# A streaming encoder trunk on one core: the memory's row statistic moved behind the key and value products, and the gated unit, one block and one opening rearranged

## The chip, the core and the metric

One Trainium2 chip, of which the kernel uses one core. The core has TensorE (PE in the profile, with its weight load PEld), VectorE (DVE), ScalarE (ACT), GpSimd (POOL) and SyncE (SP), which issues the transfers. The metric is the time of one execution on the device in microseconds (us), as the median of several runs.

## What is computed

Two layers on 512 tokens of width 1024, all in float32. Layer 0 feeds two branches from one projection (a diagonal complex state space followed by a gated linear unit, and a causal convolution followed by a LayerNorm). Layer 1 is an attention over chunks of 64. Each layer is followed by a cross attention with 4 heads into 256 memory tokens. The parts that the change touches:

```python
def rms_norm(x, g):
    y = xf * lax.rsqrt(jnp.mean(xf * xf, axis=-1, keepdims=True) + EPS)
    return (y * g).astype(x.dtype)

def s5_mixer(u, ...):
    ...
    y = y.reshape(bsz, L, S5_WIDTH) + d_skip * uf
    z = jax.nn.gelu(y)
    return z * jax.nn.sigmoid(z @ glu_w + glu_b)          # glu_w: 512 x 512

def mem_cross_attention(h, mem_n, w_qg, w_kv, w_o):
    q, g = jnp.split(h @ w_qg, 2, axis=-1)
    k, v = jnp.split(mem_n @ w_kv, 2, axis=-1)            # mem_n: 256 x 1024, k and v 256 x 1024 each
    ...

def reference(x, mem, mem_norm_g, ...):
    mem_n = rms_norm(mem, mem_norm_g)
    for layer in range(DEPTH):
        ...
        x = x + ssm_conv_layer(...)  or  chunk_attention_layer(...)
        x = x + mem_cross_attention(rms_norm(x, xa_norm_g[layer]), mem_n, ...)
    return rms_norm(x, final_norm_g)
```

## The kernel before

Activations lie with the width on the 128 partitions and the tokens in the free dimension: a width of 1024 is eight tiles of 128x512, memory eight tiles of 128x256.

**Products.** Nearly every large product takes float32 operands apart into a high part in fp32r and a rest (`split`, L173: the cast to the high part on ACT, the subtraction that gives the rest on POOL, or on the engine that is handed in). `weights` (L178) loads a weight tile through one of three `raw` buffers and splits it into one of two `whi` and one of three `wlo` buffers. `mm3` (L192) then multiplies high by high, high by low and low by high, so that a projection of 1024 rows onto 128 columns (`proj`, L201) is 24 matmuls, the sixteen on `whi` first and the eight on `wlo` after them. Two places use native float32 matmuls instead (`whole`, L187): the gated unit and three of layer 0's eight key tiles (`NATIVE`, L705). The trace writes each native matmul as two records. All matmuls are issued at L82.

**PSUM.** Banks are handed out by tag (L127): three for `proj`, two for `att`, two for `tr`, one for `acc`. A matmul group that takes a bank waits until what was in it has been read.

**Layer 0** is a list of stages (`PLAN`, L706), each a letter and a number: u is a state block's input, z and c the gate and value of a convolution block, g one of eight gates, a, b, o the preparation, scan and output of a state block, k the convolution's taps on DVE for block 0 (four a stage, L823, in a `proj` bank that stays taken throughout), v the taps of blocks 1 to 3 on PE (also in a `proj` bank), m and n the sums and the statistic of memory, l and s the LayerNorm's. The list sets priorities. Within it the scheduler may let an instruction pass another on its engine. `state_input(3)` (L865) is u3; `conv_input(2)` (L805) is c2.

**End of layer 0** (L927 to L977). `zs` are the four inputs of the gated unit. `mem_norm` (L632) spreads the memory's row statistic over the partitions (`bcast`, a matmul of `dg` with `ones` into the `acc` bank), loads the memory a second time, multiplies it by the statistic on DVE, and splits it. Then come the gated unit (four groups of four native matmuls; sigmoid on ACT, product with `zs` on POOL, product with the gate on DVE, split on POOL), the LayerNorm's application (`ln_apply`), and the key and value tiles of cross attention 0 (`kv_units`, L663; order in `KVORDER`, L704: a key tile is one weight tile, a value tile two), then the output projection (`residual`).

**Layer 1.** The chunk attention's projections (`od_qkg_d`, `unit`) are generators that are run between the steps of the attention; PE's order there is pinned. Its opening runs the first two units, takes the row statistic of x after the first (`norm["rs"]`, `dg` on DVE), spreads it with a matmul after the second (`rb_tile`, L279 copies it on ACT), and multiplies queries and keys by it before the first scores. After the chunk attention `mem_norm` runs once more for cross attention 1.

Of the kernel before, what the change touches and what calls it, by code (L numbers as in the profile page):

```python
# [44 lines left out]
def kernel(  # L45
# [578 lines left out]
    def mem_load():  # L624
        st = Stats(MEM)
        for i in range(KT):
            t = tl("mt", (P, MEM))
            nc.sync.dma_start(t, memT_d[i])
            st.add(t, pin=True)
        return st  # L630

    def mem_norm(rs, tag, raw_tag=None):  # L632
        mm, raw = [], []
        with tc.high_priority():
            rbm = bcast(rs, MEM)
# [935 lines left out]
```

## Time and profile before

| what | value |
|---|---|
| median of 3 runs | 984.75 us (981.59 to 985.48) |
| the profiled execution | 984.45 us |
| its span, first to last instruction | 982.5 us |
| mean granted clock of TensorE in it | 0.987 |
| busy: PE, PEld | 948.6 us (97%), 809.9 us (82%) |
| busy: DVE, ACT, POOL | 582.6 us (59%), 467.8 us (48%), 441.2 us (45%) |
| moved by DMA | 110.05 MB, mean 112 GB/s |

An engine is busy while it runs an instruction; waiting is the rest. PE's share is an upper bound of its work, since a matmul that runs slowly under a lowered clock is busy for longer. "Granted clock" is the share of full speed that the chip allowed TensorE in a stretch, 1.00 being 2.4 GHz and 0.50 being 1.2 GHz. Rows of a timeline give start, duration, engine, line, operation, output and inputs, shape and count; in brackets the idle time of that engine just before the row, with what ended it.

### The profile page before, as it was taken

The page shows a single profiled execution, that of the slowest core. Times are in us where ns is not written, and L with a number is a line of the kernel's source. Part 1 is how long each engine was busy: PE and PEld are TensorE (multiplying, and loading weights), DVE is VectorE, ACT ScalarE, POOL GpSimd, SP SyncE. Part 2 cuts the span into 40 slices and gives each one's busy share as a digit, 9 for nine tenths or more (in the row PEclk, how much of TensorE's full clock was granted, in tenths as well). Part 3 has the DMA queues.
Part 4 walks back from the last instruction along what each step waited for, and adds up shares of the span by engine and source line. Part 5 has one row for each costly group of instructions (what it writes and reads, how often), then busy time and mean ns, then how long its engine had stood idle before and what let it go on. Part 6 is the DMA issues. An engine that isn't in the chain of part 4 may idle for free.

```text
span 982.5 us, 14196 instructions
## 1 busy us (share of the span) xinstructions
PE 948.6 (97%) x5256; PEld 809.9 (82%) x5256; DVE 582.6 (59%) x1404; ACT 467.8 (48%) x844; POOL 441.2 (45%) x245
## 2 busy tenths in 40 slices
PE   8998999989999999999999999999999999999996
PEld 7787989758888888888798887878788998888895
DVE  7999746883344343552568777688667313433476
ACT  7243446474443434434366555656545443343352
POOL 1013343059676344457454434444327983434241
PEclk9998999999999999999999999999999999999998
DMA  8253555356422222122222222222114552122153
GB/s 294 100 163 111 166 178 179 101 166 230 161 97 90 82 70 81 65 96 89 84 77 86 82 74 70 75 79 72 65 45 139 171 179 101 65 86 85 44 171 109
DMA packets 50245, 110.05 MB, mean 112 GB/s; under 512 B 11137, under 2 KB 22529, under 8 KB 50177
## 3 DMA queue, kind: packets, MB, share of 16 engines
q1 hardware_dynamic: 49888, 109.07, 33.2%
q8 instruction: 41, 0.67, 0.3%
q14 instruction: 28, 0.22, 0.1%
q10 hardware_dynamic: 288, 0.08, 0.0%
HBM read 103.37 MB, written 5.77 MB: 111 GB/s over the span
## 4 chain that ended last, share of the span: by engine, by line
PE 34%; DVE 10%; ACT 3%; issue 2%; POOL 1%; DMA 1%; POOLq 0%; DVEq 0%; ACTq 0%
PE ps_proj L82 27%; PE ps_att L82 2%; PE ps_tr L85 2%; DVE pe L159 2%; DVE ps_att L1301 1%; PE ps_acc L82 1%; DVE o L154 1%; ACT whi L174 1%; DVE h L163 1%; PE ps_tr L82 1%; ACT pe L1288 1%; POOL wlo L154 1%; DVE z L154 1%; DVE s L1300 1%; DVE qk L154 1%
## 5 line engine op out<-in xcount | busy, mean ns | idle before, releaser
L154 POOL TENSOR_TENSOR wlo<-raw,whi 128x1024 fp32r<-128x1024 f32 x130 | 317.1, 2443 | 412.3 <-ACT whi L174 378.5
L82 PE MATMUL ps_proj<-h,whi 128*128 128x512 f32 x1184 | 301.7, 400 | 5.6 <-DVE x L154 3.3
L82 PEld LDWEIGHTS ps_proj<-h,whi 128*128 128x128 f32 x1184 | 220.6, 191 | 51.5 <-issue 8.0
L174 ACT CAST whi<-raw 128x1024 fp32r<-128x1024 f32 x148 | 155.2, 1049 | 192.2 <-PE ps_proj L82 87.0
L82 PE MATMUL ps_proj<-h,wlo 128*128 128x512 f32 x592 | 151.5, 393 | 0.0
L82 PE MATMUL ps_proj<-og,whi 128*128 128x512 f32 (+1 forms) x672 | 134.9, 347 | 0.5 <-DVE og L154 0.5
L82 PEld LDWEIGHTS ps_proj<-h,wlo 128*128 128x128 f32 x592 | 110.7, 189 | 23.0 <-issue 0.5
L82 PEld LDWEIGHTS ps_proj<-og,whi 128*128 128x128 f32 x672 | 107.6, 188 | 18.0 <-DVE og L154 2.0
L82 PE MATMUL ps_proj<-og,wlo 128*128 128x512 f32 (+1 forms) x344 | 73.4, 348 | 0.1
L82 PEld LDWEIGHTS ps_proj<-og,wlo 128*128 128x128 f32 x344 | 56.1, 188 | 8.8 <-POOL wlo L154 0.4
L154 DVE TENSOR_TENSOR pt<-ps_tr,pt 128x512 fp32r<-128x512 f32 (+1 forms) x80 | 39.9, 526 | 34.8 <-ACT pt L174 34.6
L174 ACT CAST pt<-ps_tr 128x512 fp32r<-128x512 f32 (+1 forms) x80 | 34.1, 460 | 48.2 <-PE ps_tr L85 48.0
L1288 ACT ACTIVATE pe<-ps_att,s 128x128 f32<-128x128 f32 (+3 forms) x64 | 33.4, 525 | 37.7 <-DVE s L168 34.0
L159 DVE TENSOR_SCALAR_CACHE_REDUCE pe<-pe,s 128x256 f32<-128x256 f32 (+3 forms) x96 | 48.5, 521 | 1.8
L154 DVE TENSOR_TENSOR kv<-ps_proj,kv 128x256 fp32r<-128x256 f32 (+1 forms) x24 | 12.3, 511 | 62.9 <-ACT kv L174 62.0
L154 DVE TENSOR_TENSOR z<-ps_proj,rb 128x512 f32<-128x512 f32 x32 | 22.0, 689 | 45.3 <-PE ps_proj L82 45.2
L154 POOL TENSOR_TENSOR sa<-sa,sq 128x512 f32<-128x512 f32 (+1 forms) x28 | 39.1, 1395 | 19.6 <-ACT sq L234 18.3
L154 DVE TENSOR_TENSOR x<-ps_proj,x 128x512 f32<-128x512 f32 (+1 forms) x38 | 22.9, 602 | 41.4 <-PE ps_proj L82 41.4
L163 DVE SCALAR_TENSOR_TENSOR h<-x,par,h 128x512 fp32r<-128x512 f32 x24 | 38.6, 1616 | 13.5 <-ACT h L253 13.5
L85 PE MATMUL ps_tr<-ident,pe 128*128 128x128 f32 x224 | 34.2, 274 | 3.3 <-DVE pe L159 2.3
L85 PEld LDWEIGHTS ps_tr<-ident,pe 128*128 128x128 f32 x224 | 26.9, 140 | 10.0 <-DVE pe L159 4.2
L82 PE MATMUL ps_proj<-whi,h 128*128 128x256 f32 x256 | 33.7, 284 | 0.0
(251 smaller groups left out, 1462.1 us busy)
## 6 DMA issues: line engine op xcount, KB each, us to landing
raw<-in_xa_qg_dram SPq DMA_DIRECT2D x32, 512.0 KB, 3.5
raw<-in_od_qkg_dram SPq DMA_DIRECT2D x24, 512.0 KB, 3.5
raw<-in_xa_o_dram SPq DMA_DIRECT2D x22, 512.0 KB, 3.5
raw<-in_w_in_dram SPq DMA_DIRECT2D x18, 512.0 KB, 4.1
raw<-in_xa_k_dram SPq DMA_DIRECT2D x16, 512.0 KB, 3.8
raw<-in_xa_v_dram SPq DMA_DIRECT2D x16, 512.0 KB, 3.5
cw<-in_cw_dram SPq DMA_DIRECT2D x24, 320.0 KB, 3.2
x<-in_xT_dram SPq DMA_DIRECT2D x16, 256.0 KB, 4.6
```

The costliest lines, as they stand in the source:

```text
L82: return self.keep(nc.tensor.matmul(*args, **kw))
L85: return self.keep(nc.tensor.transpose(*args))
L154: (eng or V).tensor_tensor(out, a, b, op=op)
L159: V.tensor_scalar(out=out, in0=in0, scalar1=s, scalar2=None, op0=op, op1=ALU.add, accum_out=small(1))
L163: V.scalar_tensor_tensor(out=out, in0=a, scalar=s, in1=b, op0=op0, op1=op1)
L174: A.copy(hi, src)
L1288: A.activation(st_["pe"][i], ps[:, c:c + n], AF.Exp, bias=nb, accum_out=st_["sums"][:, i:i + 1])
L1300: V.reduce_max(init, ps[:, :nf], axis=AX.X)
L1301: V.tensor_tensor_reduce(out=ps[:, nf:n], in0=ps[:, nf:n], in1=st["tz"][:, MEM - (n - nf):], scale=1.0, scalar=init, op0=ALU.add, op1=ALU. ...
```

## The change

It has six parts. **Memory** keeps no normalised copy: the tiles are loaded once for layer 0, two to a transfer, and split with the gain alone in a new stage `w0`. The row statistic is applied to the keys, one multiplication of 128x256 on DVE before the split (`kt`), and to the values, as a scalar of each token's row inside the split. For layer 1 the tiles are loaded once more and split, with no statistic. **The gated unit and the three native key tiles** use `weights` and three products; the unit's weights are split on DVE, its inputs are split too (`zp`), and its first product runs on DVE. **The order**: two value and four key tiles (`KVFIRST`) stand ahead of the unit, and the rests of layer 0's key and value weights alternate between POOL and DVE. **u3** takes a bank of `tr`. **The chunk opening**: the first three units' rests come from DVE, and the matmul that spreads the statistic is issued behind the second unit's 16th matmul. **`zs`** is written in place.

```diff
@@ proj
-    def proj(w, act, n=SEQ, cuts=()):
-        ps = psum("proj")
+    def proj(w, act, n=SEQ, cuts=(), tag="proj"):
+        ps = psum(tag)
@@ mem_load, mem_norm
-    def mem_norm(rs, tag, raw_tag=None):
...
-                t = tl("mt", (P, MEM))
-                nc.sync.dma_start(t, memT_d[i])
-                tt(t, rbm, t, ALU.mult)
...
+    def mem_load(tag, st=None):
+        tiles = []
+        for i in range(0, KT, 2):
+            t = tl(tag, (P, 2, MEM))
+            nc.sync.dma_start(t, memT_d[i:i + 2].rearrange("i p s -> p i s"))
+            for e in range(2):
+                if st is not None:
+                    st.add(t[:, e], pin=True)
+                tiles.append(t[:, e])
+        return tiles
+
+    def mem_parts(tiles, his, los):
+        mm = []
+        for i, t in enumerate(tiles):
+            if i % 2 == 0:
+                hi, lo = rl(his[i // 2], (P, 2, MEM)), rl(los[i // 2], (P, 2, MEM))
+            mm.append(gsplit(t, pc("mem_g", i), hi[:, i % 2], lo[:, i % 2]))
+        return mm
@@ kv_units
-            if ("k", i) in native:
-                w = whole(xa_k_d[layer, i])
...
+            ps = proj(weights(xa_k_d[layer, i], eng=eng()), mm, n=MEM)
             e = rl("kv", (P, 2, MEM))
+            t = tl("kt", (P, MEM))
             with tc.high_priority():
-                split(ps[:, :MEM], e[:, 0], e[:, 1], V)
+                tt(t, ps[:, :MEM], mem["rb"], ALU.mult)
+                split(t, e[:, 0], e[:, 1], V)
...
             with tc.high_priority():
-                split(ps.rearrange("p (m c) -> p m c", m=2), hi, lo, V)
+                for t in range(2):
+                    c = slice(t * MEM, (t + 1) * MEM)
+                    gsplit(ps[:, c], mem["rs"][:, t:t + 1], hi[:, t], lo[:, t])
@@ layer 0
-    KVORDER = [('k', 2), ('k', 0), ('k', 1), ('v', 3), ('k', 4), ('v', 0), ('k', 6), ('k', 3), ('k', 5), ('v', 2), ('v', 1), ('k', 7)]
-    NATIVE = [('k', 0), ('k', 1), ('k', 2)]
-    PLAN = "... a2 m0 g4 b2 v3 v3 v3 v3 g5 o2 a3 b3 n0 g6 l0 s0 o3 g7"
+    KVFIRST = [('v', 0), ('k', 0), ('k', 1), ('v', 1), ('k', 2), ('k', 3)]
+    KVORDER = [('v', 2), ('k', 4), ('k', 5), ('v', 3), ('k', 6), ('k', 7)]
+    PLAN = "... a2 m0 g4 b2 w0 v3 v3 v3 v3 g5 o2 a3 b3 n0 g6 l0 s0 o3 g7"
-        ps = proj(weights(w_in_d[3], eng=V), h0) if i == 3 else third if i == 2 else first_ps[i]
+        ps = proj(weights(w_in_d[3], eng=V), h0, tag="tr") if i == 3 else third if i == 2 else first_ps[i]
...
+        rb = bcast(mem["rs"], MEM)
+        mem["rb"] = sm.tile([P, MEM], F32, name="rbm")
+        A.copy(mem["rb"], rb)
+
+    def mem_split(i):
+        mem["mm"] = mem_parts(mem.pop("x"), ["ev"] * 4, ["uu", "x", "x", "x"])
@@ end of layer 0
-    mm, mraw = mem_norm(mrs, "og", "uu")
+    run, kv0 = kv_units(0, mem["mm"], (G, V))
+    for kind, i in KVFIRST:
+        run[kind](i)
...
+    zp = [split(t, rl("og"), rl("og"), V) for t in zs]
     for i in range(4):
-        w = whole(glu_w_d[i], 4)
-        ps = psum("proj")
-        for k in range(4):
-            T.matmul(ps, w[:, k, :], zs[k], start=(k == 0), stop=(k == 3))
-        sg = tl("ev")
+        ps = proj(weights(glu_w_d[i], kt=4, eng=V), zp)
+        sg = tl("sq")
         A.activation(sg, ps, AF.Sigmoid, bias=pc("glu_b", i))
-        tt(sg, zs[i], sg, ALU.mult, G)
-        o = tl("ev")
+        tt(sg, zs[i], sg, ALU.mult)
+        o = gates[i]
...
@@ chunk attention
+            if at is not None and i == at[0]:
+                at[1]()
...
-            for t in unit(od_qkg_d[1], h, keep):
+            def wide():
+                norm["rb"] = rb_tile(norm["rs"])
+
+            for t in unit(od_qkg_d[1], h, keep, eng=V, at=(15, wide)):
                 yield t
-            norm["rb"] = rb_tile(norm["rs"])
...
-            return ("g", hp), unit(od_qkg_d[3 * hp + 2], h, finish)
+            return ("g", hp), unit(od_qkg_d[3 * hp + 2], h, finish, eng=None if hp else V)
@@ layer 1
-    mm, _ = mem_norm(mrs, "q")
+    with tc.high_priority():
+        mm = mem_parts(mem_load("kv"), ["q"] * 4, ["q"] * 4)
```

Instructions of the whole program go from 4547 to 4736 rows on PE, 1265 to 1284 on DVE, 717 to 720 on ACT, 246 to 232 on POOL and 281 to 265 on SP.

**VectorE ahead of c2's eviction** (`x_1028<-ps_proj_1003,ev_938`, which frees the `proj` bank that gate 2 takes next). `ev_938` is z2's eviction, `m_977` to `m_980` the scan of state block 0, L163 on `ps_proj_562` a tap of convolution block 0. Before:

```order
L154 TENSOR_TENSOR ev_938<-ps_proj_913,rb_382 128x512
L163 SCALAR_TENSOR_TENSOR ps_proj_562<-tv_406,tw_118,ps_proj_562 128x512
L154 TENSOR_TENSOR m_977<-ps_att_942,cs_899 128x512
...
L590 SCALAR_TENSOR_TENSOR m_978<-d_111,m_977 128x512
L591 SCALAR_TENSOR_TENSOR m_980<-d_111,m_979 128x512
L154 TENSOR_TENSOR m_977<-m_978,cs_899 128x512
L154 TENSOR_TENSOR m_979<-m_980,cs_900 128x512
L154 TENSOR_TENSOR x_1028<-ps_proj_1003,ev_938 128x64x8
L154 TENSOR_TENSOR m_989<-m_978,cs_900 128x512
```

After:

```order
L154 TENSOR_TENSOR ev_938<-ps_proj_913,rb_382 128x512
L163 SCALAR_TENSOR_TENSOR ps_proj_562<-tv_406,tw_118,ps_proj_562 128x512
L154 TENSOR_TENSOR w_102<-g_954,g_953 64x16x16
...
L154 TENSOR_TENSOR m_977<-ps_att_942,cs_899 128x512
...
L585 SCALAR_TENSOR_TENSOR m_978<-d_111,m_977 128x512
L586 SCALAR_TENSOR_TENSOR m_980<-d_111,m_979 128x512
L154 TENSOR_TENSOR m_977<-m_978,cs_899 128x512
L154 TENSOR_TENSOR x_1028<-ps_proj_1003,ev_938 128x64x8
L154 TENSOR_TENSOR m_979<-m_980,cs_900 128x512
```

One multiplication (`m_979`) now stands behind the eviction, and of the taps of block 0 twelve instead of fourteen stand ahead of it.

**TensorE at the end of layer 0.** `ps_proj_1932` and `ps_proj_1955` are gate 7, `ps_acc_1982` spreads memory's statistic, `ps_proj_2054` and `ps_proj_2306` are the first group of the gated unit, `ps_proj_2157` a native key tile, `ps_proj_2199` value tile 3, `ps_acc_2121` and `ps_acc_2413` the LayerNorm's statistic. Before:

```order
L82 MATMUL ps_proj_1932<-h_160,wlo_1929 128x512
L82 MATMUL ps_proj_2054<-uu_1959,raw_2052 128x512
...
L82 MATMUL ps_acc_1982<-dg_1979,ones 128x256
...
L82 MATMUL ps_proj_2157<-uu_1988,raw_2155 128x256 x2
...
L82 MATMUL ps_acc_2121<-dg_2116,ones 128x512
...
L82 MATMUL ps_proj_2199<-whi_2202,og_1987 128x256 x2
```

After (`ps_proj_2000` is value tile 0, `ps_proj_2246` key tile 3, `ps_proj_2445` value tile 2, `ps_att_1927` the output of state block 3):

```order
L82 MATMUL ps_proj_1955<-h_160,wlo_1952 128x512
L82 MATMUL ps_proj_2000<-whi_2003,ev_1595 128x256
L82 MATMUL ps_proj_2000<-whi_2003,uu_1596 128x256
...
L82 MATMUL ps_att_1927<-hh_109,w_101 128x128
...
L82 MATMUL ps_proj_2246<-ev_1613,wlo_2243 128x256 x2
L82 MATMUL ps_proj_2306<-og_2284,whi_2302 128x512
...
L82 MATMUL ps_acc_2413<-dg_2408,ones 128x512
L82 MATMUL ps_proj_2445<-whi_2448,ev_1595 128x256
```

Six key and value tiles now lie between gate 7 and the gated unit, which reads split operands; memory's `dg` matmul stands in the stage n0, far ahead.

**TensorE at the chunk opening.** `ps_proj_4330` and `ps_proj_4424` are the second unit, `ps_acc_4360` and `ps_acc_4446` the matmul that spreads the statistic, `ps_att` the first scores. Before:

```order
L82 MATMUL ps_proj_4330<-h_4256,whi_4326 128x512
L82 MATMUL ps_proj_4330<-h_4207,wlo_4327 128x512
...
L82 MATMUL ps_proj_4330<-h_4255,wlo_4327 128x512
L82 MATMUL ps_acc_4360<-dg_4355,ones 128x512
L82 MATMUL ps_proj_4388<-h_4207,whi_4384 128x512
...
L82 MATMUL ps_att_4418<-qk_4373,qk_4365 128x128
```

After:

```order
L82 MATMUL ps_proj_4424<-h_4350,whi_4420 128x512
L82 MATMUL ps_acc_4446<-dg_4441,ones 128x512
L82 MATMUL ps_proj_4424<-h_4301,wlo_4421 128x512
...
L82 MATMUL ps_proj_4424<-h_4349,wlo_4421 128x512
L82 MATMUL ps_proj_4482<-h_4301,whi_4478 128x512
...
L82 MATMUL ps_att_4512<-qk_4467,qk_4459 128x128
```

The matmul that spreads the statistic moved ahead of the second unit's eight on `wlo`; between it and the first scores there are now eight matmuls more.

## Rows read from the trace of the kernel before

**Rows 1.** The page, part 1: engine, busy us, share, instructions.

```profile
PE 948.6 (97%) x5256; PEld 809.9 (82%) x5256; DVE 582.6 (59%) x1404; ACT 467.8 (48%) x844; POOL 441.2 (45%) x245
```

**Rows 2.** Timeline of PE around u3: start, us, instruction, idle before.

```profile
40.73 5.50 PE L82 MATMUL ps_proj<-h,whi 128*128 128x512 f32 x16 [2.35 <-DVE ang L154]
```

**Rows 3.** Timeline of DVE in the same stretch.

```profile
39.91 0.67 DVE L154 TENSOR_TENSOR ev<-ps_proj,rb 128x512 f32<-128x512 f32 x1
...
47.39 1.23 DVE L154 TENSOR_TENSOR wlo<-raw,whi 128x1024 fp32r<-128x1024 f32 x1 [1.50 <-ACT whi L174]
```

**Rows 4.** Timeline of PE at gate 2.

```profile
91.09 6.39 PE L82 MATMUL ps_proj<-h,whi 128*128 128x512 f32 x16 [3.28 <-DVE x L154]
```

**Rows 5.** Timeline of DVE ahead of gate 2.

```profile
84.38 1.22 DVE L590 TENSOR_TENSOR_SCAN m<-d,m 128x512 f32<-128x512 f32 x1
85.52 3.30 DVE L591 TENSOR_TENSOR_SCAN m<-d,m 128x512 f32<-128x512 f32 x1
...
89.93 1.01 DVE L154 TENSOR_TENSOR x<-ps_proj,ev 128x512 f32<-128x512 f32 x1
...
93.18 0.74 DVE L163 SCALAR_TENSOR_TENSOR ps_proj<-tv,tw,ps_proj 128x512 f32<-128x512 f32 x1
```

**Rows 6.** Timeline of POOL in that stretch.

```profile
85.03 2.71 POOL L154 TENSOR_TENSOR wlo<-raw,whi 128x1024 fp32r<-128x1024 f32 x1 [2.77 <-ACT whi L174]
```

**Rows 7.** Windows, 90 to 95 us: busy per engine, clock, DMA share, GB/s.

```profile
90.00:95.00 5.00, 3.91 (x9) 3.14 (x10) 5.00 (x9) 1.52 (x6) 0.00 (x0) 0.50 0.68 225
```

**Rows 8.** Timeline of PE, gated unit to output projection.

```profile
189.50 5.31 PE L82 MATMUL ps_proj<-uu,raw 128*128 128x512 f32 x12
...
202.45 5.40 PE L82 MATMUL ps_proj<-uu,raw 128*128 128x512 f32 x16 [1.17 <-DMA raw<-in_glu_w_dram]
208.66 2.00 PE L82 MATMUL ps_proj<-uu,raw 128*128 128x256 f32 x8 [0.81 <-ACT uu L647]
211.78 1.12 PE L82 MATMUL ps_acc<-dg,ones 128*128 128x512 f32 x2 [1.13 <-DVE mt L154]
212.75 7.07 PE L82 MATMUL ps_proj<-uu,raw 128*128 128x256 f32 x32
...
226.67 1.20 PE L82 MATMUL ps_proj<-wlo,og 128*128 128x256 f32 x8 [2.01 <-POOL wlo L154]
...
247.25 2.05 PE L82 MATMUL ps_proj<-whi,og 128*128 128x256 f32 x16
...
250.08 2.05 PE L82 MATMUL ps_proj<-whi,og 128*128 128x256 f32 x16
...
258.57 2.00 PE L82 MATMUL ps_proj<-og,whi 128*128 128x512 f32 x8
260.41 1.08 PE L82 MATMUL ps_proj<-og,wlo 128*128 128x512 f32 x4
```

**Rows 9.** Windows, 180 to 260 us: busy of PE, PEld, DVE, ACT, POOL.

```profile
180.00:260.00 80.00, 74.80 (x463) 61.57 (x463) 45.57 (x83) 46.06 (x71) 48.80 (x23) 1.00 0.50 163
```

**Rows 10.** Groups on DVE by shape: total us, mean ns, idle before.

```profile
L154 DVE TENSOR_TENSOR wlo<-raw,whi 128x1024 fp32r<-128x1024 f32 x18 | 22.8, 1265 | 4.5 <-ACT whi L174 3.6 <-PE ps_att L82 0.6 <-issue 0.2
...
L154 DVE TENSOR_TENSOR kv<-ps_proj,kv 128x256 fp32r<-128x256 f32 x16 | 6.7, 420 | 24.7 <-ACT kv L174 23.9 <-POOL sa L154 0.9
```

**Rows 11.** Timeline of DVE and POOL in the stage of rows 8.

```profile
218.33 1.05 DVE L154 TENSOR_TENSOR ev<-x,gate 128x512 f32<-128x512 f32 x1
...
223.55 3.07 POOL L154 TENSOR_TENSOR wlo<-raw,whi 128x1024 fp32r<-128x1024 f32 x1
...
224.71 2.77 DVE L154 TENSOR_TENSOR ev<-x,gate 128x512 f32<-128x512 f32 x1
```

**Rows 12.** Timeline of PE at the first scores of the chunk opening.

```profile
481.48 0.30 PE L82 MATMUL ps_att<-qk,qk 128*128 128x128 f32 x1 [1.71 <-ACT qk L1191]
```

**Rows 13.** Windows, 481 to 484 us.

```profile
481.00:484.00 3.00, 2.27 (x9) 2.14 (x10) 1.69 (x2) 0.95 (x2) 0.85 (x1) 0.69 0.00 0
```

**Rows 14.** Timeline of PE where layer 1 spreads memory's statistic.

```profile
727.04 0.70 PE L82 MATMUL ps_acc<-dg,ones 128*128 128x256 f32 x2 [0.18 <-DVE o L154]
```

More of the change, by code (lines that the diff above doesn't have):

```diff
@@ L661, in token_major, with kv_units, eng @@
                                      stop=(e == 1 and low == 1 and t % 2 == 1 and k == 3))
-    def kv_units(layer, mm, raw=None, native=()):
-        def keys(i):
-            if ("k", i) in native:
-                w = whole(xa_k_d[layer, i])
-                ps = psum("proj")
-                for j in range(KT):
-                    T.matmul(ps[:, :MEM], w[:, j, :], raw[j], start=(j == 0), stop=(j == KT - 1))
-            else:
-                ps = proj(weights(xa_k_d[layer, i]), mm, n=MEM)
+    def kv_units(layer, mm, engs=(None,)):
+        count = [0]
+        def eng():
+            count[0] += 1
+            return engs[count[0] % len(engs)]
+        def keys(i):
+            ps = proj(weights(xa_k_d[layer, i], eng=eng()), mm, n=MEM)
             e = rl("kv", (P, 2, MEM))
+            t = tl("kt", (P, MEM))
             with tc.high_priority():
-                split(ps[:, :MEM], e[:, 0], e[:, 1], V)
+                tt(t, ps[:, :MEM], mem["rb"], ALU.mult)
+                split(t, e[:, 0], e[:, 1], V)
             kk[i] = (e[:, 0], e[:, 1])
@@ L679, in values @@
             ps = psum("proj")
[L680 to L688 removed]
+            token_major([ps[:, :MEM], ps[:, MEM:]], mm, [xa_v_d[layer, h, e] for e in range(2)], eng)
             with tc.high_priority():
[L690 removed]
+                for t in range(2):
+                    c = slice(t * MEM, (t + 1) * MEM)
+                    gsplit(ps[:, c], mem["rs"][:, t:t + 1], hi[:, t], lo[:, t])
             vv[h] = (hi, lo)
@@ L921, in ln_scale @@
         lst.rs = lst.done(1.0 / 512)
-    stages = {"u": state_input, "z": conv_gate, "c": conv_input, "a": prep, "b": scan, "o": out, "g": gate, "m": mem_sums, "n": mem_scale, "v": conv_taps, "k": conv_sums,
+    stages = {"u": state_input, "z": conv_gate, "c": conv_input, "a": prep, "b": scan, "o": out, "g": gate, "m": mem_sums, "n": mem_scale, "w": mem_split, "v": conv_taps, "k": conv_sums,
               "l": ln_centre, "s": ln_scale, "t": tables}
@@ L1031, in products, with unit @@
         return prods + [(al, bh) for (ah, al), (bh, bl) in terms]
-    def unit(wsrc, act, finish, last=None, tag="whi", cols=slice(0, SEQ)):
-        wh, wl = weights(wsrc, tag=tag)
+    def unit(wsrc, act, finish, last=None, tag="whi", cols=slice(0, SEQ), eng=None, at=None):
+        wh, wl = weights(wsrc, tag=tag, eng=eng)
         n = cols.stop - cols.start
@@ L1200, in keep @@
                 late.append(ps)
-            for t in unit(od_qkg_d[0], h, keep):
+            for t in unit(od_qkg_d[0], h, keep, eng=V):
                 yield t
```

58 lines of the change are left out of this document (11 added, 47 removed).

## Prediction

> **What bounds the kernel now.** I read the page's busy shares first, then PE's timeline gap by gap, then at each gap the engine that PE waited for, and last the windows, for the clock. TensorE is busy for 948.6 of 982.5 us [rows 1], so the end is set by PE, and only two things can move it: fewer or cheaper matmuls, and the gaps with what they do to the clock. The gaps sit in few places. At u3 PE stands still for 2.35 us [rows 2]. The waits view names an angle table on DVE, but that was not the cause: PE starts at 40.73, just behind the end of z0's eviction at 39.91 + 0.67 = 40.58 [rows 3], which frees the third `proj` bank. At gate 2 it stands for 3.28 us until c2's eviction, 89.93 + 1.01 [rows 4, 5]. A gap costs more than its length. Sixteen matmuls of 128x512 take some 3.9 us at the usual pace of 0.23 each (8 from 258.57 to 260.41 [rows 8], plus the last one's tail); the sixteen behind these two gaps took 5.50 and 6.39 [rows 2, 4], while the granted clock was 0.50, the lower level, from 90 to 95 us [rows 7].
>
> **A: u3 in a `tr` bank.** No `tr` bank is in use there, so PE no longer waits for z0, only for the cast of its weights. Locally that gives 2.35 us and 5.50 - 3.9 = 1.6 us. It does not arrive at the end as it stands, because the next gap is DVE's: between 38 and 94 us DVE pauses once, for 1.50 us [rows 3], and PE would only be earlier at gate 2 and wait longer. So A is worth what c2's eviction moves up. The pause of 1.50 us was for a cast that waits until PE has read u3's weights; with PE some 4 us earlier it goes. Two taps at 0.74 [rows 5] and one multiplication of the same size, priced alike, now stand behind the eviction: 2.2. Together 3.7 us. The second scan there took 3.30 instead of 1.22 us [rows 5] beside a POOL split of 2.71 [rows 6]. Both move up, by different amounts, so whether they still meet is open: 2.1 us if not, nothing if so, another 2.1 lost if two meet. I take 0.6, a third of the gain, since only one of the two scans was hit. **A = -4.3 us**, between -1.6 (3.7 less another hit) and -8.3 (3.7 + 2.1 + the 2.5 us that the clock costs at gate 2, if that gap closes). The product of state block 0 that now stands ahead of gate 2 on PE reads what was ready before the scan; it costs nothing.
>
> **B: the end of layer 0**, from 189.50 to 258.57, 69.1 us [rows 8].
> - *Cheaper matmuls.* The gated unit's 16 native matmuls are 32 records; 12 took 5.31 us [rows 8], some 0.43 each, so 13.8 in all. In three products they are 48 at 0.23, 11.0: -2.8. The native keys' 48 records of 128x256 go at 7.07 / 32 = 0.22 [rows 8], 10.6 in all. A tile in three products takes 250.08 - 247.25 = 2.83 [rows 8], three take 8.5: -2.1. Together -4.9 us.
> - *Gaps that lose their cause.* 1.17 for the unit's weights, 0.81 for the scaled memory, 1.13 for the multiplied memory (nothing but memory's splits is needed now, and those are made in the stages before), 2.01 for a POOL rest [rows 8]: -5.1 us. What hides the unit's inputs is new: six tiles ahead of it, 4 x 2.83 + 2 x 5.66 = 22.6 us of PE.
> - *DVE's load.* It worked 45.6 of 80 us in 180 to 260 [rows 9]. It gains eight rests at 1.27 [rows 10], 10.1; four rests of the unit's weights, four of its inputs and four products, all 128x512, at 0.74 [rows 5], 8.9; eight multiplications of keys at 0.42 [rows 10], 3.4; and the values' halves, 0.6. It loses memory's sixteen instructions of 128x256, 6.7, of which about half comes back ahead of gate 7. That is 62 of some 72 us, up from 57%.
> - *New gaps.* A rest on DVE stands in one queue with evictions, LayerNorm and products, so some tile will wait for its rest. No row shows the new queue. The nearest are the waits for a rest and for a multiplication in this very stage, 2.01 + 1.13 [rows 8]: I take +3, between 0 and +10, where the whole gain is gone.
>
> DVE beside POOL is where the price can go wrong. The same DVE product of two operands took 1.05 us and, beside a POOL split, 2.77 [rows 11]. The Trainium skill, "SBUF — State Buffer", section "Who interferes with whom", states that a DVE instruction with two SBUF inputs contends with a GpSimd instruction that reads SBUF. That speaks against putting every other rest on DVE while POOL makes its neighbour; the trace agrees, with 2.77 against 1.05, and the second rival is what it would do here. The Trainium skill, "FP8 and Floating Point Precision", section "TensorE Precision Notes", gives true FP32 four passes. By it three products would save a quarter of 24.4, 6.1 us instead of 4.9, and the sum would be 1.2 lower; the rows (0.86 against 3 x 0.23) show less than four passes' worth, and I go by them.
>
> **B = -4.9 - 5.1 + 3 = -7.0 us**, between 0 and -10.
>
> **C: the chunk opening.** PE waits 1.71 us for the first queries [rows 12], and the clock is 0.69 in the 3 us around it [rows 13], 0.9 us lost. The matmul that spreads the statistic comes eight matmuls earlier, 1.8 us; the chain behind it (copy on ACT, two multiplications on DVE, casts on ACT) now waits for the second unit's last matmul instead, so I count 1.4. The three rests on DVE fall between earlier instructions and wait for nobody; if one falls into the chain it takes back 1.27 [rows 10]. **C = -1.4 - 0.9 = -2.3 us**, between -0.2 and -2.6.
>
> **D: memory in layer 1.** The matmul there goes, 727.04 to about 727.4 with 0.18 of idle ahead [rows 14]: **-0.5 us**. The keys' eight extra multiplications (8 x 0.42 [rows 10]) lie on a DVE that has room, as do memory's splits in the stages of layer 0: ahead of them PE has value tile 0, 5.7 us, that needs only weights and those splits. Were that cover gone, DVE's 3 us would show. Sixteen fewer issues on SP and one fewer read of memory take nothing from the path; the new early weight loads pass the last layer-0 weights on SP's queue, where the next load is due every 2.8 us at the fastest. `zs` in place is free.
>
> **Sum.** -4.3 - 7.0 - 2.3 - 0.5 = -14.1 us against the profiled execution, 982.5 us of span and 984.45 in all, which is 0.3 below the median: 970.3 us.
>
> **Rivals.**
> 1. *u3's gain is given back at gate 2.* For: DVE is without a pause there. Against: two taps and a product are plainly gone from ahead of the eviction. A = 0: 974.6 us.
> 2. *DVE takes PE's place at the end of layer 0.* From 62 us nominal it needs only 10 more. POOL keeps some 23 us of work there (48.8 [rows 9] less eight rests at 2.71 [rows 6] and four products at 1.05 or more [rows 11]), and a meeting doubles a DVE instruction and more [rows 11]. From half of them meeting, the stage is as long as before: B = 0, 977.4 us; up to 982 with rival 1 on top. Against: a POOL that yields is slower itself (3.07 us here [rows 11]) and spares DVE.
> 3. *Slower.* All 23 us meet: DVE needs 62 + 23 = 85 where the window had 80, +5, and four gaps open, one for every second tile that DVE feeds. If each costs the clock's 2.5 us as at gate 2, another +10. B = +15, the rest as forecast: 992.4 us. It decides from there that PE waits for DVE tile by tile. Against: tiles whose rests come from POOL let PE run on, and PE has six tiles' cover.
> 4. *Every gap closes.* A = -8.3, B = -10, C = -2.6, D = -0.5: 963.0 us.
>
> **How the numbers follow.** Forecast (966 to 973) 0.47; rival 1 0.16; rival 2 0.21, about half of it on either side of 979.8; rival 3 0.04; rival 4 0.12. A measurement of this kernel tells about 0.5%, 4.9 us, from no change: below 979.8 is faster, above 989.7 slower. Faster 0.85, same 0.11, slower 0.04. From 963 to 979.5 us leaves out half of rival 4, half of rival 2 and rival 3, some 2 in 10.
>
> **What would show it.** A: u3's matmuls start within 0.3 us of the statistic's matmul at about 38.4, and gate 2 starts by 87. If it starts at 91, A failed. B: from gate 7's end to the output projection no gap of PE above 1 us, and DVE busy below 9 of 10 us there; if DVE is full in these windows and PE's gaps are for rests or `kt` on DVE, rival 2 has it. C: the first scores start with under 0.5 us of idle and a clock of 1.00. D: no `ps_acc` with `dg` of 128x256 in the attention. What would make all of it wrong: new gaps in stages that I count as untouched, or a clock below 1.00 over a stretch without gaps.

## The result, and the profile after

The changed kernel takes 975.97 us (median; 975.6 to 979.05) against 983.57 for the kernel before in the same comparison: a ratio of 0.9923 [0.9897, 0.9948], or -7.6 us (-5.1 to -10.1). That is faster and inside the range, but about half of the 14.1 us that the sum had. The profiled execution below is the longest of its four, 979.05 us with a span of 977.3.

Part 1 of the page of after stands against [rows 1] (engine, busy us, share, instructions):

```profile
PE 942.8 (96%) x5294; PEld 814.5 (83%) x5294; DVE 625.0 (64%) x1433; ACT 478.0 (49%) x857; POOL 422.9 (43%) x233
```

PE lost 6 us of work and gained 38 records, DVE gained 42 us. Where the time went is read by setting the start of the same matmul group in both traces side by side:

| place (start on PE, us) | before | after | lead |
|---|---|---|---|
| statistic's matmul ahead of u3 | 37.35 | 35.49 | 1.86 |
| gate 2 | 91.09 | 87.36 | 3.73 |
| taps of block 1, first wait for `cw` | 131.72 | 127.07 | 4.65 |
| first matmul of the output projection | 258.57 | 259.70 | -1.13 |
| cross attention 0, sums of `sa` | 309.49 | 309.33 | 0.16 |
| behind the chunk opening | 494.92 | 492.25 | 2.67 |
| ahead of the removed matmul of layer 1 | 725.42 | 722.91 | 2.51 |
| behind it | 727.39 | 724.18 | 3.21 |
| first key tile of cross attention 1 | 761.00 | 757.67 | 3.33 |
| inside cross attention 1 | 785.94 | 780.70 | 5.24 |
| end of the span | 982.5 | 977.3 | 5.2 |

The lead of 1.86 us at the first place isn't the change's: PE has the same instructions up to there (last section). Four stretches remain. A (u3 to the taps) brought 2.8, B (taps to the sums of `sa`, that is the end of layer 0) **lost 4.5** where the forecast had -7.0, C brought 2.5, and D, with all of layer 1's memory, 2.6.

**A.** PE's timeline of after (start, us, instruction; in brackets idle before and what ended it):

```profile
35.49 1.02 PE L82 MATMUL ps_acc<-dg,ones 128*128 128x512 f32 x2
35.95 4.24 PE L82 MATMUL ps_tr<-h,whi 128*128 128x512 f32 x16
...
71.33 1.11 PE L85 MATMUL ps_tr<-ident,w 128*128 128x128 f32 x4 [2.81 <-DVE w L154]
...
87.36 3.06 PE L82 MATMUL ps_proj<-h,whi 128*128 128x512 f32 x7 [1.46 <-DVE x L154]
```

u3 stands right behind the statistic's matmul, and its sixteen take 4.24 instead of 5.50 us [rows 2]. Gate 2 starts at 87.36, near the forecast's 87, but 1.86 of its lead of 3.73 were there ahead of u3. A rest of the gap is left, 1.46 of 3.28 us [rows 4], and there is a new gap of 2.81 us at the transposes. Both have one cause, seen on DVE and POOL in the same stretch:

```profile
67.00 0.41 DVE L154 TENSOR_TENSOR w<-m,m 64x256 f32<-64x256 f32 x1
...
68.65 2.34 POOL L154 TENSOR_TENSOR wlo<-raw,whi 128x1024 fp32r<-128x1024 f32 x1 [12.84 <-ACT whi L174]
69.10 2.17 DVE L154 TENSOR_TENSOR w<-m,m 64x256 f32<-64x256 f32 x1
...
82.85 2.97 POOL L154 TENSOR_TENSOR wlo<-raw,whi 128x1024 fp32r<-128x1024 f32 x1 [2.57 <-ACT whi L174]
83.60 2.77 DVE L154 TENSOR_TENSOR m<-m,cs 128x512 f32<-128x512 f32 x1
```

The 64x256 product takes 2.17 us beside POOL's rest; the same one takes 0.41 at 67.00. The multiplication by `cs` takes 2.77; three like it at 87.16 take 1.87 together. Whether DVE's instructions here still meet POOL's was what the prediction left "open"; they do, two other ones than before.

**B.** PE's timeline at the end of layer 0, all waits from 200 us on, to be held against [rows 8]:

```profile
203.61 1.74 PE L82 MATMUL ps_acc<-ones,sa 128*128 128x1 f32 x8 [1.78 <-DVE sa L154]
...
236.29 0.39 PE L82 MATMUL ps_proj<-ev,whi 128*128 128x256 f32 x1 [2.59 <-ACT whi L174]
...
239.93 1.22 PE L82 MATMUL ps_proj<-ev,wlo 128*128 128x256 f32 x8 [1.47 <-DVE wlo L154]
...
245.48 0.36 PE L82 MATMUL ps_proj<-whi,ev 128*128 128x256 f32 x1 [1.50 <-ACT og L174]
...
251.00 1.21 PE L82 MATMUL ps_proj<-wlo,ev 128*128 128x256 f32 x8 [0.54 <-POOL wlo L154]
...
255.81 1.21 PE L82 MATMUL ps_proj<-ev,wlo 128*128 128x256 f32 x8 [1.71 <-DVE wlo L154]
```

The four gaps that the change was to remove are gone; in their place stand six of 9.6 us in all, and around the first the clock is at 0.69 (windows: busy of PE, PEld, DVE, ACT, POOL, then the clock):

```profile
200.00:210.00 10.00, 8.22 (x46) 8.02 (x45) 7.34 (x18) 4.74 (x6) 1.65 (x2) 0.69 0.23 66
180.00:260.00 80.00, 69.46 (x479) 64.36 (x478) 69.38 (x100) 47.74 (x70) 31.28 (x13) 0.96 0.40 133
```

DVE is busy for 69.4 of 80 us, 87%, but not evenly. From 220 to 250 us it has 28.5 of 30, above the nine tenths that the prediction set as the sign of a full DVE, while PE works 24.4 (columns as above):

```profile
220.00:250.00 30.00, 24.44 (x168) 22.09 (x167) 28.49 (x28) 19.57 (x29) 15.92 (x7) 1.00 0.45 151
```

DVE, POOL and ACT in that stretch show what fills it:

```profile
228.20 2.85 POOL L154 TENSOR_TENSOR wlo<-raw,whi 128x1024 fp32r<-128x1024 f32 x1
228.83 3.10 DVE L154 TENSOR_TENSOR gate<-sq,gate 128x512 f32<-128x512 f32 x1
...
231.96 0.62 ACT L174 CAST og<-gate 128x512 fp32r<-128x512 f32 x1 [4.62 <-DVE gate L154]
...
235.03 1.04 DVE L154 TENSOR_TENSOR gate<-sq,gate 128x512 f32<-128x512 f32 x1
...
235.21 1.03 ACT L174 CAST whi<-raw 128x1024 fp32r<-128x1024 f32 x1
...
238.20 1.67 DVE L154 TENSOR_TENSOR wlo<-raw,whi 128x1024 fp32r<-128x1024 f32 x1
238.74 3.38 POOL L154 TENSOR_TENSOR wlo<-raw,whi 128x1024 fp32r<-128x1024 f32 x1
...
239.79 3.19 DVE L154 TENSOR_TENSOR gate<-x,gate 128x512 f32<-128x512 f32 x1
```

A product of 1.04 us (235.03 and 243.90 in the same stretch) takes 3.10 and 3.19 beside a POOL rest, and the POOL rest itself 2.85 and 3.38, where the median of its kind in this trace is 2.40. The gap at 236.29 shows how far such a meeting reaches: the profile names ACT's cast `whi`; but ACT had stood for 4.62 us before 231.96, waiting for the stretched product, with that cast queued a few instructions behind.

**C.** At the chunk opening, to be held against [rows 12]:

```profile
479.43 0.63 PE L82 MATMUL ps_att<-qk,qk 128*128 128x128 f32 x2
...
480.71 0.44 PE L82 MATMUL ps_att<-sq,qk 128*128 128x128 f32 x2 [0.65 <-POOL sq L154]
```

The first scores start without a wait. One of 0.65 us follows for a rest on POOL.

**D.** SP's queue ahead of cross attention 1 in the kernel before (start, time to the last issue, load):

```profile
744.54 0.33 SPq L180 DMA_DIRECT2D raw<-in_xa_k_dram  x1
744.92 2.34 SPq L638 DMA_DIRECT2D mt<-in_memT_dram  x2
...
756.26 10.48 SPq L180 DMA_DIRECT2D raw<-in_xa_k_dram  x3
```

The same queue in after:

```profile
723.96 7.61 SPq L623 DMA_DIRECT2D kv<-in_memT_dram  x4
...
739.50 28.42 SPq L180 DMA_DIRECT2D raw<-in_xa_k_dram  x7
```

Before, key weights (`raw`) and memory loads took turns, and the key weights came late. In after, memory's four loads are all issued before the first key's. PE in the kernel before also had two waits for a POOL rest there, which after doesn't have:

```profile
766.44 1.21 PE L82 MATMUL ps_proj<-q,wlo 128*128 128x256 f32 x8 [0.48 <-POOL wlo L154]
770.48 1.22 PE L82 MATMUL ps_proj<-q,wlo 128*128 128x256 f32 x8 [0.91 <-POOL wlo L154]
```

### The profile page after: what moved, and what is told of

The parts are those of the page before. It is cut to its first block, busy times and chain, and to the rows that moved or that the text cites. A ratio compares the mean times of both kernels' runs of the same rounds, so it can differ in the third digit from the quotient of the medians.

```text
span 977.3 us, 14282 instructions
## 1 busy us (share of the span) xinstructions
PE 942.8 (96%) x5294; PEld 814.5 (83%) x5294; DVE 625.0 (64%) x1433; ACT 478.0 (49%) x857; POOL 422.9 (43%) x233
## 4 chain that ended last, share of the span: by engine, by line
PE 38%; DVE 9%; ACT 2%; issue 2%; POOL 0%; POOLq 0%; DVEq 0%; ACTq 0%
PE ps_proj L82 31%; PE ps_att L82 2%; PE ps_tr L85 2%; DVE pe L159 2%; DVE ps_att L1294 1%; PE ps_acc L82 1%; PE ps_tr L82 1%; DVE o L154 1%; ACT pe L1281 1%; DVE z L154 1%; DVE s L1293 1%; ACT whi L174 1%; DVE qk L154 1%; DVE g L163 0%; DVE o L163 0%
## 5 line engine op out<-in xcount | busy, mean ns | idle before, releaser
L154 POOL TENSOR_TENSOR wlo<-raw,whi 128x1024 fp32r<-128x1024 f32 x122 | 299.0, 2453 | 436.1 <-ACT whi L174 389.9
L82 PE MATMUL ps_proj<-h,whi 128*128 128x512 f32 x1168 | 294.5, 397 | 1.5 <-DVE x L154 1.5
L82 PEld LDWEIGHTS ps_proj<-h,whi 128*128 128x128 f32 x1168 | 215.9, 189 | 45.1 <-DVE x L154 1.6
L174 ACT CAST whi<-raw 128x1024 fp32r<-128x1024 f32 (+1 forms) x155 | 160.7, 1038 | 166.9 <-PE ps_proj L82 82.1
L82 PE MATMUL ps_proj<-og,whi 128*128 128x512 f32 (+1 forms) x624 | 132.1, 358 | 0.0
L82 PEld LDWEIGHTS ps_proj<-og,whi 128*128 128x128 f32 x624 | 104.3, 188 | 17.5
L82 PEld LDWEIGHTS ps_proj<-og,wlo 128*128 128x128 f32 x320 | 54.1, 188 | 9.3 <-POOL wlo L154 0.2
L154 DVE TENSOR_TENSOR wlo<-raw,whi 128x1024 fp32r<-128x1024 f32 (+1 forms) x33 | 43.1, 1307 | 14.2 <-ACT whi L174 13.8
L163 DVE SCALAR_TENSOR_TENSOR h<-x,par,h 128x512 fp32r<-128x512 f32 x24 | 40.4, 1689 | 14.7 <-ACT h L248 14.7
L154 POOL TENSOR_TENSOR sa<-sa,sq 128x512 f32<-128x512 f32 (+1 forms) x28 | 41.9, 1497 | 14.5 <-ACT sq L229 14.1
```

Source lines behind the costliest of these rows:

```text
L82: return self.keep(nc.tensor.matmul(*args, **kw))
L154: (eng or V).tensor_tensor(out, a, b, op=op)
L163: V.scalar_tensor_tensor(out=out, in0=a, scalar=s, in1=b, op0=op0, op1=op1)
L174: A.copy(hi, src)
```

## Experiments

Theories on B, the failed part. **Load**: DVE has too much to do, so less work on it helps. **Contention**: POOL's rests and DVE's two-operand instructions slow each other, so *more* on DVE and less on POOL helps. **Order**: what is late is late by its place in the queues, so neither matters. **Products**: the three-product unit, with eight more splits, isn't worth it.

| kernel | us | ratio to before | taps to sums of `sa` |
|---|---|---|---|
| before | 982.6 to 983.6 | 1 | 177.8 |
| after | 975.97 | 0.9923 [0.9897, 0.9948] | 182.3 |
| 1, key/value rests on POOL | 980.97 | 0.9978 [0.9963, 0.9994] | 185.4 |
| 2, key/value rests on DVE | 968.43 | 0.9850 [0.9826, 0.9873] | 172.0 |
| 3, u3 alone | 979.20 | 0.9962 [0.9946, 0.9978] | 178.9 |
| 4, after with native unit | 976.27 | 0.9929 [0.9904, 0.9953] | 180.2 |
| 5, opening alone | 979.32 | 0.9952 [0.9933, 0.9972] | 178.3 |
| 6, layer 1's memory alone | 981.19 | 0.9981 [0.9963, 0.9998] | |
| 7, as 2, unit's rests on DVE too | 965.76 | 0.9811 [0.9788, 0.9834] | 170.3 |
| 8, as 2 with native unit | 968.58 | 0.9840 [0.9816, 0.9864] | 172.6 |
| 9, as 7 with idle POOL work | 977.15 | 0.9950 [0.9935, 0.9966] | 181.3 |
| 10, before with rests on DVE | 982.58 | 1.0005 [0.9996, 1.0014] | 176.5 |
| 11, as 7 with native unit | 967.02 | 0.9841 [0.9825, 0.9857] | 169.9 |
| 12, as 7, layer 0 on DVE too | 961.78 | 0.9799 [0.9780, 0.9819] | |

The last column is one stretch of PE in the trace, from the taps' first wait for `cw` to cross attention 0's sums of `sa`. Experiments 3 and 5 have before's instructions there and read 178.9 and 178.3, so a difference of 1 us in this column shows nothing.

### 1 and 2: who makes the rests of keys and values

```diff
-    run, kv0 = kv_units(0, mem["mm"], (G, V))
+    run, kv0 = kv_units(0, mem["mm"], (G,))      # 1
+    run, kv0 = kv_units(0, mem["mm"], (V,))      # 2
```

> The changed kernel with all rests of layer 0's key and value weights on POOL; DVE loses eight rests, about 10 us, at the end of layer 0. Changed kernel: 976.0 us. Load theory (DVE has too much work there, whoever runs beside it): the gaps of PE between gate 7 and the output projection, 10.5 us in the changed kernel's trace, fall to under 5 and the time to 968 to 972. Contention theory (DVE instructions of two operands meet POOL's rests and take two to three times as long): twice as many rests to meet, DVE's gain is eaten, 974 to 980, gaps 8 us or more. Order theory (what is late is late by where it stands in the queues): within 1.5 us of 976.

> The changed kernel with all rests of layer 0's key and value weights on DVE; DVE gains eight rests, about 10 us, and POOL has no rest to make in that stage. Load theory: the gaps grow by 5 to 10 us, 981 to 986. Contention theory: the stretched instructions (3.1 to 3.4 us for products that take 1.05, 3.40 for a rest that takes 1.22) fall back to their own length, which gives back about what the eight rests cost: 972 to 978. Order theory: within 1.5 us of 976.

Taking eight rests from DVE made the kernel 5.0 us slower than after, giving it eight more made it 7.5 faster. Both lie just outside the ranges given for contention, by 1.0 us above and 3.6 below, but on its side; the order theory's 1.5 us falls with them. Load falls: with eight rests fewer, some 10 us, DVE was busy 67.4 us instead of 69.4, since the others stretched; with eight more it was busy 70.6. PE in experiment 1 has gaps behind POOL and behind DVE alike:

```profile
244.06 1.21 PE L82 MATMUL ps_proj<-ev,wlo 128*128 128x256 f32 x8 [1.92 <-POOL wlo L154]
...
248.13 0.55 PE L82 MATMUL ps_proj<-whi,ev 128*128 128x256 f32 x1 [2.85 <-DVE kv L163]
```

The window of 180 to 260 us in experiment 1 (columns as above):

```profile
180.00:260.00 80.00, 68.91 (x461) 64.10 (x460) 67.37 (x93) 46.34 (x68) 46.61 (x20) 0.91 0.39 126
```

The same window in experiment 2, where PE is busy for 77 us at full clock:

```profile
180.00:260.00 80.00, 77.15 (x524) 69.54 (x523) 70.58 (x112) 51.11 (x75) 15.18 (x7) 1.00 0.50 160
```

### 7 and 9: POOL quiet, and POOL busy with nothing

Experiment 7 also moves the last POOL work of the stretch, the rests of the unit's results. Experiment 9 then adds twenty POOL subtractions of finished key and value tiles, whose results nobody reads; all else is as in 7.

```diff
-        yg[i] = split(o, rl("og"), rl("og"))
+        yg[i] = split(o, rl("og"), rl("og"), V)      # 7 and 9
...
+                d = tl("h", (P, 2, MEM))             # 9, after each of ten tiles
+                for _ in range(2):
+                    tt(d, f(t), f(t), ALU.subtract, G)
```

> The second run's kernel (968.4 us, all rests of layer 0's key and value weights on DVE) with the rests of the gated unit's results on DVE as well, so that POOL is idle from gate 7 to the output projection. Contention theory: the last stretched products (1.75, 2.33, 1.78 and 1.69 us) fall back to 1.05 to 1.22, some 3 us, against four more instructions of 0.7: 966.5 to 968.5. Load theory: 970 to 972.

> The seventh run's kernel (965.8 us, POOL without work from gate 7 to the output projection) with twenty POOL subtractions of 128x512 added, two behind each of the first ten key and value tiles; they read the finished tile and their result is used by nothing. PE, DVE and ACT have the same instructions in the same order. Contention theory: some 26 us of POOL work stretch what they meet on DVE, which is 9 of 10 us busy there; 970 to 980, with DVE products and rests of 2 us and more again. Load theory and order theory: DVE's work and every queue are unchanged, 965.8 within 1 us.

The window of 180 to 240 us in experiment 7:

```profile
180.00:240.00 60.00, 59.93 (x434) 55.48 (x434) 55.41 (x100) 41.87 (x62) 0.00 (x0) 1.00 0.44 142
```

The same window in experiment 9:

```profile
180.00:240.00 60.00, 56.84 (x398) 52.38 (x397) 57.23 (x95) 38.87 (x56) 18.25 (x13) 0.97 0.41 127
```

The row of 7 to hold against that of after, 220 to 250 us:

```profile
220.00:250.00 30.00, 29.27 (x219) 27.57 (x218) 30.00 (x38) 20.99 (x30) 5.36 (x2) 1.00 0.63 200
```

With POOL at 0, PE works 59.9 of 60 us while DVE does 55.4, more than in after (50.4). The idle POOL work cost 11.4 us between the medians (13.7 by the ratios), and 11.0 in the stretch of the table's last column. PE, DVE and ACT have the same instructions in 9 in the same order, up to cross attention 0, and PE waits for DVE, not for POOL (PE's timeline of 9):

```profile
247.74 1.22 PE L82 MATMUL ps_proj<-ev,wlo 128*128 128x256 f32 x8 [2.17 <-DVE wlo L154]
...
256.33 3.54 PE L82 MATMUL ps_proj<-og,whi 128*128 128x512 f32 x8 [3.59 <-DVE kt L154]
```

DVE in 9 beside six of the subtractions:

```profile
234.37 1.22 DVE L154 TENSOR_TENSOR wlo<-raw,whi 128x1024 fp32r<-128x1024 f32 x1
...
237.80 10.79 POOL L154 TENSOR_TENSOR h<-kv 128x512 f32<-128x512 f32 x6 [18.30 <-ACT kv L248]
...
238.97 0.41 DVE L154 TENSOR_TENSOR kv<-kt,kv 128x256 fp32r<-128x256 f32 x1
...
239.70 0.40 DVE L154 TENSOR_TENSOR kt<-ps_proj,rbm 128x256 f32<-128x256 f32 x1
...
241.28 1.26 DVE L154 TENSOR_TENSOR kv<-kt,kv 128x256 fp32r<-128x256 f32 x1
...
245.67 2.02 DVE L154 TENSOR_TENSOR wlo<-raw,whi 128x1024 fp32r<-128x1024 f32 x1
```

The rest of a weight tile took 1.22 us ahead of POOL's row and 2.02 in it, the rest of a key tile 0.41 at its beginning (spans on POOL are rough) and 1.26 further in. `kt`, of the same size but with one of its inputs in a PSUM bank, kept 0.40. Here only the load of the neighbour differs, so this shows the contention by itself. It also sets aside a rival of experiments 1 and 2, that a rest takes 2.4 us on POOL and 1.2 on DVE and is late for that alone: no key or value tile needs what POOL makes here.

### 4, 8 and 11: the unit native again

```diff
-    zp = [split(t, rl("og"), rl("og"), V) for t in zs]
...
-        ps = proj(weights(glu_w_d[i], kt=4, eng=V), zp)
+        w = tl("raw", (P, 4, P))
+        nc.sync.dma_start(w, glu_w_d[i])
+        ps = psum("proj")
+        for k in range(4):
+            T.matmul(ps, w[:, k, :], zs[k], start=(k == 0), stop=(k == 3))
```

> The changed kernel with the gated unit's product as native float32 matmuls again (its inputs and weights are not split: 5.5 us less on DVE, 2.8 us more on PE by the durations of before). Load theory: gaps fall by 4 us or more, 973 to 976. If the three products were a plain gain for PE and DVE had room: 979. Order theory: 977 to 979.

> The second run's kernel (968.4 us) with the gated unit's product as native float32 matmuls again, not split. If PE sets the stage there, the native matmuls cost what the prediction gave for them, 2.8 us: 971.2. If DVE still sets it, DVE's 5.5 us less are worth more than PE's 2.8: 966 to 968.5.

> The seventh run's kernel (965.8 us) with the gated unit's product as native float32 matmuls again. In that kernel PE is busy for 59.9 of 60 us from 180 to 240, so there the prediction's price of three products against native ones should show in full: 2.8 us more, 968.6. If DVE still sets the stage: 964 to 966.

Beside after and beside 2 the native unit costs 0.3 and 0.15 us, beside 7 it costs 1.3 (2.9 by the ratios; their intervals overlap). The unit's matmuls in 11:

```profile
210.32 13.89 PE L82 MATMUL ps_proj<-uu,raw 128*128 128x512 f32 x32
```

In 7 they run from 210.16 to 221.79, 11.6 us. So the 2.3 us are there, but 7 has two gaps, 0.73 and 0.88 us at the output projection, that 11 doesn't have. That the eight splits on DVE open them is likely and was not tested.

### 3, 5 and 6: the other parts alone, on the kernel before

```diff
...
-        ps = proj(weights(w_in_d[3], eng=V), h0) if i == 3 else ...
+        ps = proj(weights(w_in_d[3], eng=V), h0, tag="tr") if i == 3 else ...      # 3
...
-            for t in unit(od_qkg_d[1], h, keep):                                     # 5
+            def wide():
+                norm["rb"] = rb_tile(norm["rs"])
...
+            for t in unit(od_qkg_d[1], h, keep, eng=V, at=(15, wide)):
...
-            norm["rb"] = rb_tile(norm["rs"])
...
-    mm, _ = mem_norm(mrs, "q")                                                       # 6
...
+        mm = mem_parts(mem_pairs("kv"), ["q"] * 4, ["q"] * 4)
```

> The kernel before with u3 in a bank of tr and nothing else. If the prediction's term holds: 4.3 us below the kernel before, 979.3 against 983.6. By the traces (a new gap of 2.81 us opened at the first transposes of state block 0, and gate 2 kept 1.46): 2 to 3 us below. If u3's gain is given back in full: within 1 us.

> The kernel before with the chunk opening of the change and nothing else. Kernel before: 983.2 us. The prediction's term: 2.3 us less, 980.9. By the traces of before and of the changed kernel, where the lead grows by 2.5 us between 463 and 495 us: 980.7. If the opening's gain were given back behind the first scores: 983.

> The kernel before with layer 1's memory as in the change (loaded two tiles to a transfer, split with the gain alone, statistic on keys and values), but the matmul that spreads the statistic kept in its place. If the prediction's price is right, layer 1 gains by that matmul alone: no change, 983.2 us. If the gain there, 2.7 us in the changed kernel's trace, comes from key weights no longer queued behind eight memory loads on SP: 1.5 to 2.5 us less, 981 to 981.7, and the two waits of PE for POOL rests at 766 and 770 us are gone.

u3 alone is worth 3.7 us by the ratio; it starts at 37.41, again without a gap, and from the statistic's matmul ahead of it to the taps its trace is 4.2 us shorter than before's. In 5 the lead over before grows from 2.68 us (460.77 against 463.45) to 5.24 (489.68 against 494.92) across the opening, by 2.6; the comparison of runs gives 4.7 (2.8 to 6.6). The trace's other lead lies where nothing was changed, and why the runs have more than 2.6 stays unexplained. Layer 1's memory alone, with the matmul that spreads the statistic kept, is worth 1.9 (0.2 to 3.6). In its trace, the longest of its twelve executions (987.53 us), the key weights follow memory in one piece as in after, and of the two waits for POOL one is left, 0.63 us.

### 10 and 12: the same remedy elsewhere

```diff
-                ps = proj(weights(xa_k_d[layer, i]), mm, n=MEM)
+                ps = proj(weights(xa_k_d[layer, i], eng=None if layer else V), mm, n=MEM)      # 10, values alike
...
-    UENG = 'VVVVVVVVVVGG'
-    GATE_V = (0, 3, 5, 7)
+    UENG = 'VVVVVVVVVVVV'                                                                       # 12
+    GATE_V = (0, 1, 2, 3, 4, 5, 6, 7)
```

> The kernel before with all rests of layer 0's key and value weights on DVE and nothing else (there DVE is 1 to 2 of 10 us busy in that stretch and the gap for a POOL rest is 2.0 us). Contention theory with room on DVE: the gap of 2.0 us goes and the stretched products of the convolution branch (2.1 to 2.8 us) fall to 1.05; 2 to 3.5 us less than before, 980 to 981.5. If the gain of the second run belongs to the new order of the stage alone: no change, 983.3.

> The seventh run's kernel (965.8 us) with the rests of gates 1, 2, 4 and 6 and of the last convolution block's weights on DVE as well, so that POOL makes no rest in all of layer 0. There DVE is busy for 53 to 55 of 60 us between 60 and 120. Contention theory alone: the remaining meetings (a multiplication of 2.77 us beside a POOL rest at 83 us in the changed kernel) go, 1 to 3 us less, 963 to 965. If DVE's load decides where it has no pause: the six rests, 7 us, show at gate 2 and behind it, 967 to 972.

In the kernel before, where DVE had 45.6 of 80 us [rows 9], the move brought nothing that can be measured, though contention had 2 to 3.5 us for it. In its trace the wait of 2.01 us for a POOL rest became one of 0.60 for a cast, and the stretch is 1.3 us shorter; why the time doesn't show it is open. Experiment 12 moves the rests of four gates and of the last convolution block's two inputs, which POOL still made. It has the lowest time: 961.78 us, 2.0% below before. Against 7 it is 4.0 us by the medians and 1.2 by the ratios, whose intervals overlap, so what these rests add is not settled. Its page:

```profile
PE 936.6 (98%) x5294; PEld 808.1 (84%) x5294; DVE 622.4 (65%) x1451; ACT 474.3 (49%) x855; POOL 379.2 (40%) x215
```

The gap at gate 2 is gone; of A's two gaps one is left, 0.92 us at the transposes. But 2 and 7 have no gap at gate 2 either, with its rests on POOL as in after, so the move is not shown to be the cause (last section).

## Why the prediction was right and where it wasn't

The time lies in the range, but not by the sum. The forecast's own span, 966 to 973, was missed; A and C came about as priced, B came out with the other sign, and the range holds 975.97 because it reached into rival 2.

**A held.** Forecast -4.3, alone -3.7 by runs (2.2 to 5.3) and -4.2 in its trace, -2.8 in the trace of after. The chain on DVE that the prediction followed (the pause goes, two taps and a product leave the queue ahead of c2's eviction) is what moved gate 2, and rival 1 fell: the gain wasn't given back. The open point, whether DVE's instructions still meet POOL's, was answered twice with yes.

**B failed**, +4.5 in the trace for -7.0. The removed gaps did go, and with POOL quiet (7) the stretch is 170.3 us against 177.8, 7.5 less, so the other terms were about right together. One was smaller: the unit's products gave 2.3 instead of 2.8 on PE, and in the stretch nothing of it shows (170.3 with them, 169.9 without). The step that failed is "New gaps: I take +3, between 0 and +10". It measured 9.6 us from 200 us on and 0.95 ahead of that, and the lowered clock, for which the term had nothing, comes on top: in 200 to 210 us PE was busy for 8.2 us at 0.69, some 3 us of work not done (an estimate: 0.31 of 10 us). With both, -4.9 - 5.1 + 10.5 + 3 is +3.5, near the +4.5 of the trace. The runs say less: the other parts alone add up to -10.3 (3.7, 4.7 and 1.9) and the whole is -7.6, which leaves +2.7 for B, each with an interval of 2 us or so. The value of 3 came from waits of the kernel before, in which a rest was late once; but there nearly all rests were POOL's and DVE had 43% of its time free. What the change built, rests by turns on POOL and DVE while DVE's products run, had no row there except the pair in [rows 11], 1.05 against 2.77. That pair was the right row, and I gave it to a rival with 0.21.

Rival 2 is what happened, in its mechanism, in its signs (DVE full from 220 to 250 us, PE's waits for rests on DVE among them) and nearly in its time (977.4; measured 975.97). The time is so near in part by chance: rival 2 had B at 0, and what B lost beyond that came back in C and D. A full DVE is not enough for it, though: 7 has DVE busy for all of 220 to 250 us, and PE works 29.3 of these 30 us instead of 24.4. What differs is what fills DVE. A product three times as long holds up the cast behind it on ACT, and that the next tile. The Trainium skill, "SBUF — State Buffer", section "Who interferes with whom", says that a DVE instruction with two SBUF inputs contends with a GpSimd instruction that reads SBUF. The runs agree: 1.04 became 3.10 and 3.19 us, and the price of idle POOL work was 11.4 us. They agree on the two inputs as well. Counted over all fourteen traces, DVE's two-operand instructions on 128x256 with both inputs in SBUF took 0.42 us at the median away from POOL's instructions (287 of them) and 1.74 beside one, that is, for four fifths of their own time or more (169); with one input in PSUM they took 0.42 in both places, and none of the 195 beside POOL more than 0.43.

The other page weighed there, "FP8 and Floating Point Precision" in the Trainium skill, section "TensorE Precision Notes", had four passes for true FP32. By it the unit's 11.6 us of three products would be 15.5 natively, an estimate. It took 13.89, a native matmul 3.6 times as long as one of a product (0.87 against 0.24 us), and the measurement decides. The prediction read its 0.86 against 3 x 0.23 as fewer than four passes; the ratio doesn't show that, since a product's matmul may take longer than a pass, and no run here separates the two.

**C held** in the traces: -2.3 forecast, -2.5 in after and -2.6 alone, the first scores without idle time. The runs of the opening alone say -4.7 (2.8 to 6.6), more than the term, for a reason that is open.

**D was mis-sized**: -0.5 forecast, -2.6 in the trace of after and -1.9 alone. That sixteen fewer issues on SP and one fewer read of memory "take nothing from the path" was wrong: memory's second load stood in SP's queue between the key weights, and the rests that followed them were late (0.48 and 0.91 us). The traces separate the two: at the removed matmul the lead grows from 2.51 to 3.21, 0.7 for the 0.5 forecast, and over the first key tiles from 3.33 to 5.24, 1.9 for a forecast of nothing.

The sum of the traced parts is -2.8 + 4.5 - 2.5 - 2.6 = -3.4; with the start's 1.86 it makes the span's 5.2. The runs say -7.6 between medians; the profiled execution is 3.1 us longer than the median of after (before's 0.9 longer than its own), which accounts for the rest. In which stretch the other executions of after save these 3 us isn't known, so each of the four terms is uncertain by some of it.

## What to carry to other kernels

To share a row of like instructions between DVE and POOL by turns isn't halving the work: in this kernel a meeting stretched the DVE instruction and often the POOL rest too, and giving all of it to DVE, though that was then busy for 55 of 60 us, was faster by 7.5 us, and by 10.2 with the unit's rests too. When a change puts POOL work beside two-operand DVE work, look in the trace before for one such pair, price every meeting by it, and follow the late instruction to what is queued behind it on the next engine. And where PE is said to wait for ACT, look at what ACT itself waited for last.

## What was not expected of the hardware

The start of an execution varies with the same instructions. The first 20 us of before (windows; the clock is the third number from the end):

```profile
0.00:10.00 10.00, 7.47 (x27) 5.64 (x28) 4.02 (x11) 5.65 (x8) 4.19 (x16) 0.88 0.82 269
10.00:20.00 10.00, 10.00 (x42) 8.05 (x41) 9.23 (x21) 9.73 (x17) 0.00 (x0) 0.94 0.95 337
```

The same of experiment 3, whose PE differs from it only from u3 on, at 37 us:

```profile
0.00:10.00 10.00, 8.47 (x28) 6.93 (x29) 4.31 (x12) 5.84 (x9) 4.20 (x16) 1.00 0.81 266
10.00:20.00 10.00, 10.00 (x43) 8.05 (x43) 9.27 (x20) 9.89 (x17) 0.00 (x0) 1.00 0.96 354
```

The granted clock was 0.88 and 0.94 in one and 1.00 in the other. The statistic's matmul ahead of u3 started between 35.49 us (after) and 38.05 (experiment 6). The four traces with a lowered clock in these 20 us (before, 2, 6 and 7) come to it at 37.35 to 38.05, the ten at 1.00 at 35.49 to 36.95; so the clock is a part of it, and the rest is open. A head start doesn't last, either: in after, 8 and 11, which come there by 35.85, the wait at the transposes is 2.81 us and gate 2's sixteen matmuls take 5.5 (9, at 35.80, has the wait and then only 3.9); in 1 and 4, which come a microsecond later, the waits are 0.43 to 0.61 and 1.4, gate 2's take 3.9, and it starts 0.5 to 1 us earlier than in the former. In 2 and 7, at 37.5, gate 2 has no gap. A shift of a microsecond or two went with which product POOL's rest met and how long it took (2.17 and 2.53 us in after and 8, 1.69 in 1 and 4); that it is the cause is likely, not tested. Differences of one or two microseconds between single traces of this kernel, A's 2.8 against 3.7 among them, are not to be explained further.
